# Inverse roots on ScalarE by logarithm and exponential, an earlier memory weight, a later key transpose and a respaced memory tail

## The chip, the cores and the metric

One core of a Trainium2 chip runs the whole kernel. The metric is device time in microseconds (us), from one launch; the median of three runs is compared. Five engines work side by side, each through its own list of instructions in order: TensorE (PE) multiplies matrices, ScalarE (ACT) applies functions to tiles, VectorE (DVE) and GpSimd (POOL) do elementwise work, and SyncE (SP) issues the transfers. An instruction that waits for another engine holds up everything behind it in its own list.

## The reference

The kernel computes one hybrid decoder layer for 1024 tokens of width 1024, with 256 memory tokens beside them:

```python
h = RMSNorm(x)                                       # x * rsqrt(mean(x^2) + 1e-6) * g
[pool_v | pool_gate | sb_q | sb_k | sb_v | sb_gate | mem_q | mem_gate] = h @ W_in
y_pool = pool_mixer(pool_v) * silu(pool_gate)        # windows 2, 4, 8, 16
y_sb   = stick_breaking(sb_q, sb_k, sb_v) * silu(sb_gate)          # 8 heads of 64
mk, mv = split(RMSNorm(mem) @ W_mem_kv)              # 4 heads of 64
s      = RMSNorm(mem_q) @ RMSNorm(mk).T / 8          # norms per head
y_mem  = softmax(s) @ mv * silu(mem_gate)
x      = x + concat(y_pool, y_sb, y_mem) @ W_out
```

Four kinds of norm need an inverse square root: of x (8 blocks of 128 tokens), of mem (2 blocks), of the memory keys and of the memory queries (per head).

## The kernel before

**Precision.** Every fp32 operand of a product is split into a high part, which ScalarE copies (`hh`, `wh_`), and the rest, which VectorE or GpSimd subtracts (`hl`, `wl_`). A product is three matmuls: high by high, low by high, high by low.

**Start.** The memory tokens are normed late (the factor `rm` is applied to the product), so the memory's keys and values `kv` can be multiplied as soon as `mem` and the first weights are there. The weights `w_mem_kv` come in four pieces, and SP issues them alternating with token blocks x0 to x3. `Norm.square` sums squares on ScalarE, `Norm.root` forms v = mean + eps on VectorE and v to the power -0.5 on GpSimd (L123), `newton` refines it by one step on VectorE, and `scale` multiplies the block. Then `h_step` transposes four blocks at once (L379, tile `tx`), so the first `tx` needs x0 to x3, and the first transposes of the second half need x4 to x7. `warm` puts unneeded matmuls into TensorE's list.

**Memory queries and keys.** Matmuls `u_mq` project the queries, for two pairs of heads and two halves of the tokens (`half[pr, th]`). `kv_root`, `kv_newton` give the keys' factor `r_k`, L447 the normed keys `kmn`, and `km_step` transposes them on TensorE (L469, tile `tk`). `mem_ss` sums squares of queries (`sp`, `v_q`, `r_q`), `mem_scale` makes the factor `qsc`. Roots of several columns go through `rsqrt_cols` (L95, on GpSimd).

**Memory attention.** `mem_main` lists 16 items (pair, head, two token blocks). Each is a score product `z_m` (L574, two tiles in turn), a maximum `nb_m` (L576, L580), the exponentials `pe_m` on ScalarE (L584), reciprocal (L592) and scaling of `pe_m` by GpSimd and VectorE (L595), a transpose `ta_m` (L493), its split `ah_m` (ScalarE, L503) and `al_m` (VectorE, L504), and the product `av` (L512). The transpose of an item comes three items after its scores, its `av` one later.

**Order.** TensorE's list is always the order of the code. `weave` mixes these steps with projections of the attention that follows (`u_k`, `u_v`, `u_g`): each step has a cost for TensorE, an occupation `occ` by which filling work is shared out, and a latency until what it gives is ready. VectorE's, ScalarE's and GpSimd's lists follow the code until `start.close()`; after that a scheduler orders them.

**After it** come four pairs of stick-breaking attention and the output product, which the change does not edit.

Of the kernel before, what the change touches and what calls it, by code (L numbers as in the profile page):

```python
# [8 lines left out]
F32 = mybir.dt.float32  # L9
F32R = mybir.dt.float32r  # L10
AF = mybir.ActivationFunctionType
# [3 lines left out]
P = 128  # L15
# [10 lines left out]
def layer_kernel(  # L26
# [48 lines left out]
    ctx.enter_context(tc.manual_schedule(engines={mybir.EngineType.PE}))  # L75


    ident = const.tile([P, P], F32, name="ident")
    make_identity(nc, ident[:])
    grow = pool.tile([P, P], F32, tag="pw", name="grow")[0:20, :]  # L80
    spare = const.tile([P, 2], F32, name="spare")
    rm = const.tile([P, 2], F32, name="rm")
    mhalf = const.tile([P, 16], F32, name="mhalf")
    nc.gpsimd.memset(mhalf[:], -0.5)
    bones = const.tile([P, 2], F32, name="bones")
    nc.gpsimd.memset(bones[:], 0.0)
    nc.gpsimd.memset(bones[0:HD, 0:1], 1.0)
# [2 lines left out]
    def rsqrt_cols(ss, n, inv, name):  # L90
        r = pool.tile([P, 16], F32, tag="rs", name=f"r_{name}", bufs=4)
        v = pool.tile([P, 16], F32, tag="rsv", name=f"v_{name}", bufs=2)
        t = pool.tile([P, 16], F32, tag="rst", name=f"t_{name}", bufs=2)
        nc.vector.tensor_scalar(v[:, :n], ss, inv, EPS, op0=ALU.mult, op1=ALU.add)
        nc.gpsimd.tensor_tensor(r[:, :n], v[:, :n], mhalf[:, :n], op=ALU.pow)  # L95

        def newton():
            nc.vector.tensor_tensor(t[:, :n], r[:, :n], r[:, :n], op=ALU.mult)
            nc.vector.tensor_tensor(t[:, :n], t[:, :n], v[:, :n], op=ALU.mult)
            nc.vector.tensor_scalar(t[:, :n], t[:, :n], -0.5, 1.5, op0=ALU.mult, op1=ALU.add)  # L100
            nc.vector.tensor_tensor(r[:, :n], r[:, :n], t[:, :n], op=ALU.mult)
            return r

        return newton

    class Norm:
# [11 lines left out]
                    sq[:], self.t, 1.0, self.t, op0=ALU.mult, op1=ALU.mult, accum_out=self.ss  # L118
                )

        def root(self):
            nc.vector.tensor_scalar(self.v, self.ss, 1.0 / D, EPS, op0=ALU.mult, op1=ALU.add)
            nc.gpsimd.tensor_tensor(self.r, self.v, mhalf[:, 0:1], op=ALU.pow)  # L123

        def newton(self, col=None):
            r, m = self.r, self.m
# [222 lines left out]
    def warm(dst, n):  # L349
        for i in range(n):  # L350
            nc.tensor.transpose(dst[:, 0:P], ident[:], ident[:])
# [17 lines left out]
    kb = [slot2(f"KB{i}", f"raw{i}") for i in range(2)]  # L369
    early_raw = [None, kb[1][:, 0:1024], kb[1][:, 1024:2048], kb[0][:, 0:1024], kb[0][:, 1024:2048], None]  # L370
    raw_kv = []
    for kk in range(4):
        raw_kv.append(load_raw(w_kv_v[:, 2 * kk : 2 * kk + 2, :], f"kv{kk}", early_raw[kk]))
        nc.sync.dma_start(xt[kk][:], xv[kk * P : (kk + 1) * P, :])

    def h_step(th, k):
        tp = ps(("z", "tr")[k % 2], f"tx{th}_{k}")
# [23 lines left out]
    def kv_split(kk):  # L401
        tags = (("wh", "wl"), ("wh", "wl"), ("qa0", "qb0"), ("KA0",))[kk]
        w_kv.append(split_w(raw_kv[kk], f"kv{kk}", tags, (nc.vector, nc.gpsimd)))

    def kv_step(kk):
        wh, wl = w_kv[kk]
        for j in range(2):
            k = 2 * kk + j
            wc = slice(j * 512, (j + 1) * 512)
            for w, m in ((wh, mh), (wh, ml), (wl, mh)):  # L410
                for i in range(2):
                    nc.tensor.matmul(
                        kvp[i][:],
                        m[:, k, i * P : (i + 1) * P],
                        w[:, wc],
                        start=(k == 0 and m is mh and w is wh),
                        stop=(k == KD - 1 and w is wl),
                    )
# [141 lines left out]
    def mem_main(mq, ys):  # L560
        items = [(pr, h, 2 * th + j) for th in range(2) for pr in range(2) for h in range(2) for j in range(2)]
        box = {}

        def qk(it):
            pr, h, j = it
            q, c0 = mq[pr][0]()[h], q_col(pr, 2 * j, h)
            rows = slice(h * HD, (h + 1) * HD)
            name = f"m{pr}_{h}_{j}"
            zp = ps("z", f"z_{name}")
            for i in range(2):  # L570
                tcol = slice((2 * j + i) * P, (2 * j + i + 1) * P)
                mc = slice(i * M, (i + 1) * M)
                for n in range(2):
                    nc.tensor.matmul(zp[:, mc], q[:, tcol], km[pr][:, 2 * n + h, :], start=(n == 0), stop=(n == 1))  # L574
            nb = pool.tile([P, 8], F32, tag="nb", name=f"nb_{name}", bufs=5)
            nc.vector.tensor_reduce(  # L576
                nb[:, 0:2], zp[:, 0:512].rearrange("p (i m) -> p i m", i=2), axis=AX.X, op=ALU.max, negate=True
            )
            pt = slot("be", f"pe_{name}")
            nc.vector.tensor_tensor(nb[:, 2:4], nb[:, 0:2], qsc[:, c0 : c0 + 3 : 2], op=ALU.mult)  # L580
            for i in range(2):
                col = c0 + 2 * i
                mc = slice(i * M, (i + 1) * M)
                nc.scalar.activation(  # L584
                    pt[:, mc],
                    zp[:, mc],
                    AF.Exp,
                    bias=nb[:, 2 + i : 3 + i],
                    scale=qsc[:, col : col + 1],
                    accum_out=nb[:, 4 + i : 5 + i],  # L590
                )
            nc.vector.reciprocal(nb[:, 6:8], nb[:, 4:6])  # L592
            for i in range(2):
                mc = slice(i * M, (i + 1) * M)
                (nc.gpsimd, nc.vector)[i].tensor_scalar_mul(pt[:, mc], pt[:, mc], nb[:, 6 + i : 7 + i])  # L595
            box[it] = pt

        def tr(it):
            pr, h, j = it
            pt = box[it]  # L600
            blocks = [[pt[:, i * M + b * P : i * M + (b + 1) * P] for i in range(2)] for b in range(2)]
            box[it] = a_t(blocks, f"m{pr}_{h}_{j}")

        def av(it):
            pr, h, j = it
            name = f"m{pr}_{h}_{j}"
            acc = av_half()
            a_v(acc, [vm[0][:, b, 2 * pr + h, :] for b in range(2)], box.pop(it), True, True)
            av_out(acc, h, name, ys[pr][h * HD : (h + 1) * HD, 2 * j * P : (2 * j + 2) * P])

        steps = []
        n = len(items)
        for t in range(n + 4):
            if t < n:
                steps.append(Step(0.44, lambda it=items[t]: qk(it), 1.5, 2.5, [("q", t - 3)], ("q", t)))
            if 0 <= t - 3 < n:
                steps.append(Step(0.43, lambda it=items[t - 3]: tr(it), 0.7, 2.4, [("q", t - 3)], ("t", t - 3)))
            if 0 <= t - 4 < n:
                steps.append(Step(0.44, lambda it=items[t - 4]: av(it), 0.3, 0.0, [("t", t - 4)]))
        return steps  # L620
# [154 lines left out]
        return Unit(r * P, f"pv{r}", evac), mix + [(KC, lambda th=th: out_step(th)) for th in range(2)]  # L775


    nc.scalar.activation(spare[:, 0:1], mhalf[:, 0:1], AF.Exp)
    start = ExitStack()
    start.enter_context(  # L780
        tc.manual_schedule(engines={mybir.EngineType.DVE, mybir.EngineType.Activation, mybir.EngineType.Pool})
# [23 lines left out]
    kv_split(0)  # L805
    m_evac(1)
    kv_step(0)
    m_evac(2)
    xn[0].square()
    kv_split(1)  # L810
    kv_step(1)
    m_evac(3)
    xn[0].root()
    xn[1].square()
    kv_split(2)
    xn[0].newton()
    xn[0].scale(nc.vector)
    kv_step(2)
    xn[1].root()
    xn[2].square()  # L820
    kv_split(3)
    xn[1].newton()
    xn[1].scale(nc.vector)
    xn[2].root()
    xn[3].square()
    xn[2].newton()
    xn[3].root()
    xn[2].scale(nc.vector)
    kv_step(3)
    for i in range(2):  # L830
        mn[i].root()
    raw_mq = [load_raw(w_in_v[:, :, 2560 + pr * P : 2560 + (pr + 1) * P], f"mq{pr}", early_raw[4 + pr]) for pr in range(2)]
    for i in range(4, 8):
        nc.sync.dma_start(xt[i][:], xv[i * P : (i + 1) * P, :])
    xn[3].newton()
    xn[3].scale(nc.vector, slice(0, 512))
    warm(ps("tr", "warm"), 4)
    w_mq = [(slot("wh", f"wh_mq{pr}", dt=F32R), slot("wl", f"wl_mq{pr}", dt=F32R)) for pr in range(2)]
    wc = (slice(0, 512), slice(512, 1024))

# [39 lines left out]
    for k in range(KD):  # L880
        half[0, 0][k][1]()
        half[1, 0][k][1]()
        if k + 3 < KD:
            h_step(0, k + 3)
        if k >= 5:
            h_step(1, k - 5)
        if k == 0:
            for i in range(2):
                mn[i].newton(col=rm[:, i : i + 1])
        if k <= 3:  # L890
            xn[4 + k].newton()
        if k < 2:
            xn[6 + k].square()
            xn[6 + k].root()
        if k <= 3:
            xn[4 + k].scale(nc.gpsimd if k < 2 else nc.vector)
        if k == 3:
            u_q[0].weights()
        if k == 4:
            kv_evac()  # L900
# [10 lines left out]
    for k in range(KD):  # L911
        half[0, 1][k][1]()
        if k == 0:
            kv_root()
            kv_newton()
        if k in (2, 3):
            mem_ss(k - 2, 0)
        if k == 4:
            mem_scale(0)
        if k in (6, 7):  # L920
            km_step(kmn, k - 6)
    for k in range(KD):
        half[1, 1][k][1]()
        if k == 1:
            u_k[0].weights()
        if k == 5:
            mem_ss(0, 1)
    start.close()
# [236 lines left out]
```

## Time and profile before

| quantity | value |
| --- | --- |
| median of 3 runs | 527.53 us (527.09 to 528.45) |
| the profiled execution, its own time | 532.06 us |
| its span, first to last instruction | 530.3 us |
| busy share: PE, DVE, ACT, POOL | 97%, 74%, 54%, 33% |
| mean granted clock of TensorE | 0.990 |

TensorE is busy nearly throughout, so the time is its work, its few waits, and the stretches in which its matmuls run slower. Times on the trace count from the start of the span. The profiled execution took 4.53 us more than the median; differences worked out on its trace are applied to the median.

### The profile page before, as it was taken

What the parts mean: (1) busy time and instruction counts of PE and PEld (TensorE: products, weight loads), DVE (VectorE), ACT (ScalarE), POOL (GpSimd) and SP (SyncE); (2) the same over time, 40 slices, a digit from 0 to 9 for tenths busy, and PEclk for the clock granted to TensorE, in tenths of its full rate; (3) what the DMA queues carried; (4) which work ended last, traced back from release to release, by engine and by line L of the source; (5) the groups of instructions that cost most, each with busy time, mean ns of one, the idle gap of its engine ahead of it and who ended that gap; (6) DMA issues with size and microseconds to landing.
All of it is one profiled execution on the core that took longest, in us unless ns stands there. A gap on an engine that the chain in (4) does not pass through costs nothing.

```text
span 530.3 us, 7458 instructions
## 1 busy us (share of the span) xinstructions
PE 515.0 (97%) x2720; PEld 433.1 (82%) x2720; DVE 393.3 (74%) x635; ACT 287.2 (54%) x549; POOL 177.0 (33%) x196
## 2 busy tenths in 40 slices
PE   7899898999899999999999999999999999999997
PEld 6678777888788888888888888888788888888886
DVE  4687667767567885876766776747988859999973
ACT  7787437667556564555545564535544539462400
POOL 3780464444122022022202210222345920034790
PEclk9999899999899999999999999999999999999999
DMA  8911012310110230123011113100110415413123
GB/s 298 339 45 41 0 54 66 81 40 1 40 41 1 80 81 0 41 58 91 13 40 41 41 40 80 40 25 19 40 41 0 159 45 195 159 41 119 41 110 127
DMA packets 37244, 37.25 MB, mean 70 GB/s; under 512 B 1990, under 2 KB 26840, under 8 KB 37208
## 3 DMA queue, kind: packets, MB, share of 16 engines
q1 hardware_dynamic: 37208, 36.78, 22.4%
q8 instruction: 21, 0.34, 0.3%
q14 instruction: 15, 0.12, 0.1%
HBM read 28.39 MB, written 4.19 MB: 61 GB/s over the span
## 4 chain that ended last, share of the span: by engine, by line
PE 85%; DVE 7%; ACT 2%; DMA 2%; POOL 2%; issue 1%; SPq 0%; ACTq 0%; POOLq 0%
PE av L512 8%; PE z L640 7%; PE ta L493 6%; PE u_g L209 6%; PE u_v L209 6%; PE u_k L209 5%; PE u_q L209 5%; PE u_g L206 3%; PE u_v L206 3%; PE u_mg L209 3%; PE oS L1047 3%; PE oS L1049 3%; PE u_pv L209 3%; PE oS L1048 3%; PE u_k L206 2%; PE u_q L206 2%
## 5 line engine op out<-in xcount | busy, mean ns | idle before, releaser
L648 DVE TENSOR_TENSOR_SCAN be<-be,later 128x128 f32<-128x128 f32 (+3 forms) x64 | 92.1, 1454 | 15.8 <-ACT be L644 14.8
L498 ACT ACTIVATE ah<-ta,mone 128x512 fp32r<-128x512 f32 (+1 forms) x80 | 51.6, 645 | 55.7 <-PE ta L493 54.9
L499 DVE SCALAR_TENSOR_TENSOR al<-ta,ah 128x512 fp32r<-128x512 f32 (+1 forms) x80 | 50.6, 632 | 23.3 <-ACT ah L498 22.2
L644 ACT ACTIVATE be<-z 128x128 f32<-128x128 f32 (+3 forms) x96 | 45.6, 490 | 32.3 <-PE z L640 30.8
L493 PE MATMUL ta<-ident,be 128*128 128x128 f32 x288 | 45.0, 273 | 0.0
L493 PEld LDWEIGHTS ta<-ident,be 128*128 128x128 f32 x288 | 34.8, 140 | 7.7 <-DVE be L648 0.7
L512 PEld LDWEIGHTS av<-ah,V_v 128*128 128x128 f32 x160 | 29.7, 188 | 6.7
L512 PE MATMUL av<-al,V_v 128*128 128x256 f32 (+1 forms) x160 | 31.7, 280 | 1.1 <-DVE al L499 1.1
L512 PE MATMUL av<-ah,V_v 128*128 128x256 f32 (+1 forms) x160 | 30.3, 271 | 0.0
L152 POOL TENSOR_TENSOR wl_k<-wr_k,wh_k 128x256 fp32r<-128x256 f32 x16 | 12.0, 782 | 47.9 <-ACT wh_k L148 47.9
L584 ACT ACTIVATE pe_m<-z_m,nb_m,qsc 128x256 f32<-128x256 f32 x32 | 17.8, 561 | 18.6 <-DVE nb_m L580 15.1
L206 PE MATMUL u_g<-hh,wh_g 128*128 128x512 f32 x64 | 27.7, 433 | 0.0
L206 PE MATMUL u_v<-hh,wh_v 128*128 128x512 f32 x64 | 27.1, 423 | 0.0
L595 POOL TENSOR_SCALAR pe_m<-pe_m,nb_m 128x256 f32<-128x256 f32 x16 | 16.9, 1056 | 29.8 <-DVE nb_m L592 25.7
L152 POOL TENSOR_TENSOR wl_g<-wr_g,wh_g 128x256 fp32r<-128x256 f32 x16 | 11.3, 741 | 45.7 <-ACT wh_g L148 30.8
L206 PE MATMUL u_k<-hh,wh_k 128*128 128x512 f32 x64 | 26.5, 414 | 0.0
L1047 PE MATMUL oS<-bs,hh 128*128 128x512 f32 (+1 forms) x68 | 25.9, 381 | 0.0
L1049 PE MATMUL oS<-bs,hl 128*128 128x512 f32 (+1 forms) x68 | 25.8, 379 | 0.0
L209 PE MATMUL u_g<-hh,wl_g 128*128 128x512 f32 x64 | 25.7, 402 | 0.0
L209 PE MATMUL u_g<-hl,wh_g 128*128 128x512 f32 x64 | 25.7, 402 | 0.0
L1048 PE MATMUL oS<-bs,hh 128*128 128x512 f32 (+1 forms) x68 | 25.6, 376 | 0.0
L209 PE MATMUL u_v<-hl,wh_v 128*128 128x512 f32 x64 | 25.3, 396 | 0.0
(312 smaller groups left out, 1497.5 us busy)
## 6 DMA issues: line engine op xcount, KB each, us to landing
x<-in_x_dram SPq DMA_DIRECT2D x8, 512.0 KB, 6.5
wr_q<-in_w_in_dram SPq DMA_DIRECT2D x4, 512.0 KB, 4.6
wr_k<-in_w_in_dram SPq DMA_DIRECT2D x4, 512.0 KB, 3.6
wr_v<-in_w_in_dram SPq DMA_DIRECT2D x4, 512.0 KB
KA_k<-KA_k SPq DMA_DIRECT2D x8, 256.0 KB, 5.4
KB_k<-KB_k SPq DMA_DIRECT2D x8, 256.0 KB, 4.6
wr_g<-in_w_in_dram SPq DMA_DIRECT2D x4, 512.0 KB, 4.7
xr<-in_x_dram SPq DMA_DIRECT2D x8, 256.0 KB, 4.6
```

The source lines that it names most:

```text
L206: nc.tensor.matmul(pt[:], wh[:, kc], hh[k][:, c], start=(k == 0), stop=False)
L209: nc.tensor.matmul(pt[:], w[:, kc], h[k][:, c], start=False, stop=(k == KD - 1 and n == 1))
L493: nc.tensor.transpose(tp[:, o : o + P], src, ident[:])
L498: nc.scalar.activation(ah[:, :w], tp[:, :w], AF.Identity, bias=mone[:, 0:1])
L499: nc.vector.scalar_tensor_tensor(al[:, :w], tp[:, :w], -1.0, f(ah[:, :w]), op0=ALU.add, op1=ALU.subtract)
L512: nc.tensor.matmul(av[:, 256 - bw : 256], vs[n], part[:, o : o + bw], start=(first and part is ah and n == 0), stop=(last and part is al a ...
L640: nc.tensor.matmul(zp[:, 0:w], q[h][:, tcol], k[h][:, n, s0 : s0 + w], start=(n == 0), stop=(n == 1))
L644: nc.scalar.activation(be[:, s0 : s0 + w], zp[:, 0:w], AF.Sigmoid, scale=-(HD**-0.5))
L648: nc.vector.tensor_tensor_scan(be[:, rev], be[:, rev], mask, 1.0, op0=ALU.mult, op1=ALU.max)
L1047: nc.tensor.matmul(bk[:, c], xh[:, tcol], wh[:, c], start=(n == 0), stop=False)
L1048: nc.tensor.matmul(bk[:, c], xh[:, tcol], wl[:, c], start=False, stop=False)
L1049: nc.tensor.matmul(bk[:, c], xl[:, tcol], wh[:, c], start=False, stop=(n == 3))
```

## The change

The dummy exponential at the start goes; instead table set 6 is loaded explicitly on ScalarE. The roots of x0 to x3, of the keys and of the queries are formed on ScalarE as exp(-0.5 ln(scale * ss + eps)), in two instructions; those of x4 to x7 and of mem stay on GpSimd. The second piece of the memory weights is issued ahead of x0, and x2 and x3 stand after the last piece. The start is written in another order, and 8 unneeded matmuls stand where 4 did. The roots of mem move from ahead of the first `u_mq` loop to its step 1, their Newton steps from step 0 to step 3. The two `km_step` calls move from the last two steps of `half[0, 1]` to steps 2 and 3 of `half[1, 1]`. In `mem_main`, transposes that come after the last scores get `occ` 2.2 instead of 0.7: 51 instead of 33 projection matmuls then stand after the last `z_m`, and 132 instead of 150 between the first and the last.

```diff
+    nc.scalar.add_instruction(
+        mybir.InstLoadActFuncSet(name=nc.get_next_instruction_name(), act_func_set_id=6, ins=[], outs=[])
+    )
...
+        nc.scalar.activation(r[:, :n], ss, AF.Ln, bias=eps[:, 0:1], scale=inv)
+        nc.scalar.activation(r[:, :n], r[:, :n], AF.Exp, scale=-0.5)
         nc.vector.tensor_scalar(v[:, :n], ss, inv, EPS, op0=ALU.mult, op1=ALU.add)
-        nc.gpsimd.tensor_tensor(r[:, :n], v[:, :n], mhalf[:, :n], op=ALU.pow)
...
-        def root(self):
+        def root(self, act=False):
+            if act:
+                nc.scalar.activation(self.r, self.ss, AF.Ln, bias=eps[:, 0:1], scale=1.0 / D)
+                nc.scalar.activation(self.r, self.r, AF.Exp, scale=-0.5)
             nc.vector.tensor_scalar(self.v, self.ss, 1.0 / D, EPS, op0=ALU.mult, op1=ALU.add)
-            nc.gpsimd.tensor_tensor(self.r, self.v, mhalf[:, 0:1], op=ALU.pow)
+            if not act:
+                nc.gpsimd.tensor_tensor(self.r, self.v, mhalf[:, 0:1], op=ALU.pow)
...
-    for kk in range(4):
+    for kk, blocks in enumerate(((), (0,), (1,), (2, 3))):
...
-                steps.append(Step(0.43, lambda it=items[t - 3]: tr(it), 0.7, 2.4, [("q", t - 3)], ("t", t - 3)))
+                steps.append(Step(0.43, lambda it=items[t - 3]: tr(it), 0.7 if t < n else 2.2, 2.4, [("q", t - 3)], ("t", t - 3)))
...
-    nc.scalar.activation(spare[:, 0:1], mhalf[:, 0:1], AF.Exp)
...
+    xn[0].root(True)
+    kv_split(2)
     m_evac(3)
...
-    warm(ps("tr", "warm"), 4)
+    warm(ps("tr", "warm"), 8)
...
-        if k == 0:
+        if k == 1:
+            for i in range(2):
+                mn[i].root()
+        if k == 3:
             for i in range(2):
                 mn[i].newton(col=rm[:, i : i + 1])
...
-        if k in (6, 7):
-            km_step(kmn, k - 6)
     for k in range(KD):
         half[1, 1][k][1]()
...
+        if k in (2, 3):
+            km_step(kmn, k - 2)
```

The first place is the start of ScalarE's list, before the change. `sq_x` sums squares of a token block, `wh_kv` copies the high part of memory weights, `mh` that of the transposed memory tokens.

```order
L115 ACTIVATE sq_x_234,ss_x_114<-x_97 128x1024
L157 ACTIVATE wh_kv_236<-raw_130 128x512 x2
L393 ACTIVATE mh<-tm_128,gcol 128x256 x2
L115 ACTIVATE sq_x_260,ss_x_115<-x_98 128x1024
L157 ACTIVATE wh_kv_262<-raw_130 128x512 x2
L115 ACTIVATE sq_x_285,ss_x_116<-x_99 128x1024
L157 ACTIVATE w_kv_287<-raw_129 128x512 x2
L115 ACTIVATE sq_x_297,ss_x_117<-x_100 128x1024
```

The same stretch of ScalarE's list after the change:

```order
L123 ACTIVATE sq_x_254,ss_x_117<-x_100 128x1024
L131 ACTIVATE ss_x_117<-ss_x_117,eps 128x1
L132 ACTIVATE ss_x_117<-ss_x_117 128x1
L169 ACTIVATE wh_kv_259<-raw_133 128x512 x2
L406 ACTIVATE mh<-tm_131,gcol 128x256 x2
L123 ACTIVATE sq_x_272,ss_x_118<-x_101 128x1024
L131 ACTIVATE ss_x_118<-ss_x_118,eps 128x1
L132 ACTIVATE ss_x_118<-ss_x_118 128x1
L169 ACTIVATE w_kv_289<-raw_132 128x512 x2
L123 ACTIVATE sq_x_297,ss_x_119<-x_102 128x1024
L131 ACTIVATE ss_x_119<-ss_x_119,eps 128x1
L132 ACTIVATE ss_x_119<-ss_x_119 128x1
```

A logarithm (L131) and an exponential (L132) of one column stand behind each sum of squares, and the second copy of memory weights has moved ahead of the first `sq_x`.

The second place is TensorE's list where the keys are transposed (`tk`). Before the change it stands in the first pair's queries:

```order
L206 MATMUL u_mq_1_602<-hh_86,wh_mq_335 128x512
L209 MATMUL u_mq_1_602<-hl_94,wh_mq_335 128x512
L209 MATMUL u_mq_1_602<-hh_86,wl_mq_336 128x512
L469 MATMUL tk_668<-ident,kmn 128x128 x2
L206 MATMUL u_mq_1_602<-hh_87,wh_mq_335 128x512
L209 MATMUL u_mq_1_602<-hl_95,wh_mq_335 128x512
L209 MATMUL u_mq_1_602<-hh_87,wl_mq_336 128x512
L469 MATMUL tk_689<-ident,kmn 128x128 x2
L206 MATMUL u_mq_1_700<-hh_80,wh_mq_337 128x512
```

After it, `tk` stands in the second pair's queries:

```order
L221 MATMUL u_mq_1_612<-hh_90,wl_mq_342 128x512
L218 MATMUL u_mq_1_688<-hh_83,wh_mq_343 128x512
...
L218 MATMUL u_mq_1_688<-hh_85,wh_mq_343 128x512
L221 MATMUL u_mq_1_688<-hl_93,wh_mq_343 128x512
L221 MATMUL u_mq_1_688<-hh_85,wl_mq_344 128x512
L482 MATMUL tk_708<-ident,kmn 128x128 x2
L218 MATMUL u_mq_1_688<-hh_86,wh_mq_343 128x512
```

Each `tk` has moved behind 12 further `u_mq` matmuls.

The third place is ScalarE's list at the end of the memory attention, where the last item's exponentials stand (`pe_m_1_3`). Before the change:

```order
L584 ACTIVATE pe_m_1_2_1401,nb_m_1_2_1399<-z_m_1_2_1394,nb_m_1_2_1399,qsc 128x256 x2
L503 ACTIVATE ah_m_1_3_1433<-ta_m_1_3_1428 128x512
L525 ACTIVATE avt_m_1_2_1445<-av_1440 64x256
L584 ACTIVATE pe_m_1_3_1458,nb_m_1_3_1456<-z_m_1_3_1451,nb_m_1_3_1456,qsc 128x256 x2
L503 ACTIVATE ah_m_0_2_1476<-ta_m_0_2_1471 128x512
L309 ACTIVATE V_v_1363<-tv_v_1_1480 128x8x64
```

After the change:

```order
L321 ACTIVATE V_v_1416<-tv_v_0_1417 128x8x64
L538 ACTIVATE avt_m_1_2_1429<-av_1424 64x256
L516 ACTIVATE ah_m_0_2_1457<-ta_m_0_2_1452 128x512
L597 ACTIVATE pe_m_1_3_1439,nb_m_1_3_1437<-z_m_1_3_1432,nb_m_1_3_1437,qsc 128x256 x2
L307 ACTIVATE vt_v_1_1464<-u_v_1_1360 128x512
L538 ACTIVATE avt_m_1_3_1473<-av_1468 64x256
```

The copy `ah_m` of item 0_2 stood behind the last exponentials and now stands ahead of them. In VectorE's list `al_m` of that item has likewise moved ahead of the last item's reciprocal. Of the 12 items from the fifth on, 8 had nothing between the maximum's last step and the reciprocal in VectorE's list; 5 have nothing there now.

## Rows read from the trace of the kernel before

**Rows 1.** Waits of PE in the whole span: line, released by; us in total, times, longest.

```profile
PE z_m L574 <- ACT pe_m L584: 2.1, 1, 2.1
PE ta_m L493 <- DVE al_m L504: 1.9, 1, 1.9
PE tk L469 <- DVE kmn L447: 1.6, 1, 1.6
PE tx L379 <- DVE x L133: 1.2, 1, 1.2
PE tx L379 <- DVE ss_m L122: 1.1, 1, 1.1
...
PE kv L412 <- ACT wh_kv L157: 0.7, 1, 0.7
```

**Rows 2.** Windows: width; busy (count) of PE, PEld, DVE, ACT, POOL; clock, DMA share, GB/s.

```profile
24.34:38.10 13.76, 13.71 (x69) 11.06 (x70) 10.87 (x29) 12.17 (x21) 11.97 (x14) 0.88 0.22 68
...
58.14:74.10 15.96, 15.95 (x71) 13.06 (x72) 8.60 (x24) 9.45 (x16) 7.98 (x6) 0.89 0.11 34
...
81.49:135.09 53.60, 53.60 (x316) 46.15 (x316) 38.55 (x92) 36.42 (x96) 24.97 (x33) 1.00 0.18 49
...
137.03:147.40 10.37, 10.37 (x53) 9.03 (x53) 4.91 (x9) 4.84 (x9) 0.02 (x1) 0.84 0.01 2
147.40:490.00 342.60, 341.42 (x1828) 288.19 (x1827) 268.59 (x371) 185.12 (x334) 85.30 (x90) 1.00 0.20 59
```

**Rows 3.** Timeline of ACT at the start: start, us, operation, idle before.

```profile
0.71 1.28 ACT L778 ACT_TABLE_LOAD   x1 [0.71 <-PEq L1152]
2.01 0.20 ACT L778 ACTIVATE spare<-mhalf 128x1 f32<-128x1 f32 x1
...
24.71 0.69 ACT L381 ACTIVATE hh<-tx,gcol 128x512 fp32r<-128x512 f32 x1 [1.94 <-PE tx L379]
```

**Rows 4.** Timeline of DVE at the start.

```profile
23.74 0.55 DVE L133 TENSOR_SCALAR x<-x,ss_x 128x512 f32<-128x512 f32 x1
...
30.42 0.27 DVE L127 TENSOR_SCALAR ss_m<-ss_m 128x1 f32<-128x1 f32 x1
...
37.23 0.81 DVE L133 TENSOR_SCALAR x<-x,ss_x 128x1024 f32<-128x1024 f32 x1
```

**Rows 5.** Timeline of PE, two matmuls that follow one another.

```profile
29.27 0.39 PE L209 MATMUL u_mq<-hl,wh_mq 128*128 128x512 f32 x1
29.51 0.39 PE L206 MATMUL u_mq<-hh,wh_mq 128*128 128x512 f32 x1
```

**Rows 6.** Timeline at the keys' root, POOL and DVE.

```profile
54.14 1.66 POOL L95 TENSOR_TENSOR r_k<-v_k,mhalf 128x8 f32<-128x8 f32 x1 [14.11 <-DVE v_k L94]
...
57.66 0.76 DVE L447 TENSOR_TENSOR kmn<-kvs,r_k 128x256 f32<-128x256 f32 x2
```

**Rows 7.** Timeline at the queries' roots, POOL and DVE.

```profile
71.85 2.90 POOL L95 TENSOR_TENSOR r_q<-v_q,mhalf 128x16 f32<-128x16 f32 x1 [3.28 <-DVE v_q L94]
74.72 2.84 POOL L152 TENSOR_TENSOR wl_v<-wr_v,wh_v 128x256 fp32r<-128x256 f32 x4
...
61.92 0.17 DVE L98 TENSOR_TENSOR t_q<-r_q 128x16 f32<-128x16 f32 x1 [3.02 <-POOL r_q L95]
...
74.78 0.70 DVE L98 TENSOR_TENSOR t_q<-r_q 128x16 f32<-128x16 f32 x1 [3.01 <-POOL r_q L95]
```

**Rows 8.** Timeline at the memory attention's end, ACT and DVE.

```profile
134.47 0.56 ACT L584 ACTIVATE pe_m<-z_m,nb_m,qsc 128x256 f32<-128x256 f32 x1 [2.17 <-PE av L512]
...
135.57 0.59 ACT L503 ACTIVATE ah_m<-ta_m 128x512 fp32r<-128x512 f32 x1
...
136.19 0.69 DVE L504 TENSOR_TENSOR al_m<-ta_m,ah_m 128x512 fp32r<-128x512 f32 x1
```

**Rows 9.** Waits of DVE from 81.49 to 135.09.

```profile
DVE nb_m L592 <- ACT pe_m L584: 11.7, 11, 1.4
DVE nb_m L576 <- PE z_m L574: 1.3, 3, 0.7
```

More of the change, by code (lines that the diff above doesn't have):

```diff
@@ L82, in layer_kernel @@
     rm = const.tile([P, 2], F32, name="rm")
-    mhalf = const.tile([P, 16], F32, name="mhalf")
+    mhalf = const.tile([P, 1], F32, name="mhalf")
     nc.gpsimd.memset(mhalf[:], -0.5)
+    eps = const.tile([P, 1], F32, name="eps")
+    nc.gpsimd.memset(eps[:], EPS)
     bones = const.tile([P, 2], F32, name="bones")
@@ L371, in layer_kernel @@
     raw_kv = []
-    for kk in range(4):
+    for kk, blocks in enumerate(((), (0,), (1,), (2, 3))):
         raw_kv.append(load_raw(w_kv_v[:, 2 * kk : 2 * kk + 2, :], f"kv{kk}", early_raw[kk]))
-        nc.sync.dma_start(xt[kk][:], xv[kk * P : (kk + 1) * P, :])
+        for i in blocks:
+            nc.sync.dma_start(xt[i][:], xv[i * P : (i + 1) * P, :])
     def h_step(th, k):
@@ L807, in layer_kernel @@
     kv_step(0)
+    kv_split(1)
     m_evac(2)
+    kv_step(1)
     xn[0].square()
-    kv_split(1)
-    kv_step(1)
+    xn[0].root(True)
+    kv_split(2)
     m_evac(3)
-    xn[0].root()
-    xn[1].square()
-    kv_split(2)
     xn[0].newton()
     xn[0].scale(nc.vector)
+    xn[1].square()
+    xn[1].root(True)
     kv_step(2)
-    xn[1].root()
-    xn[2].square()
     kv_split(3)
@@ L823, in layer_kernel @@
     xn[1].scale(nc.vector)
-    xn[2].root()
+    xn[2].square()
+    xn[2].root(True)
+    kv_step(3)
+    xn[2].newton()
     xn[3].square()
-    xn[2].newton()
-    xn[3].root()
+    xn[3].root(True)
     xn[2].scale(nc.vector)
-    kv_step(3)
-    for i in range(2):
-        mn[i].root()
     raw_mq = [load_raw(w_in_v[:, :, 2560 + pr * P : 2560 + (pr + 1) * P], f"mq{pr}", early_raw[4 + pr]) for pr in range(2)]
```

## The prediction

> **What bounds the kernel now.** I read the list of TensorE's waits first, since TensorE is the engine that hardly ever rests. In the longest window, 342.60 us of stick-breaking attention, it is busy for 341.42 us [rows 2]. The change edits nothing there, so what is won or lost before 147 us reaches the end. Only the first 147 us matter.
>
> Two things cost there. The first is waits: the list shows 2.1 us for a third `z_m`, 1.9 for a `ta_m`, 1.6 for a `tk`, 1.2 and 1.1 for two `tx`, and 0.7 for a `kv` [rows 1]. The second shows only in the windows. Three stretches have a granted clock of 0.88, 0.89 and 0.84, though TensorE is nearly 100% busy in them [rows 2]: width times the missing share is 13.76 x 0.12 = 1.65 us, 15.96 x 0.11 = 1.76 us and 10.37 x 0.16 = 1.66 us. Each is a short piece at 1.2 GHz among work at 2.4 GHz. The windows begin where a wait ends: for the last `tx`, the `tk`, the `ta_m`. The 2.1 us wait of `z_m` ended at 81.49, and the window behind it shows 1.00. So a wait was followed by a slow piece in three of four places, and I can't tell from the rows what spared the fourth.
>
> **The price of the new operation.** No row shows a logarithm with a bias on one column. The nearest is the one-column exponential at 2.01, 0.20 us [rows 3]; two of these make 0.40, which is the lower end. The upper end is two 512-column copies with a factor per partition, 0.69 each, so 1.38 [rows 3]. I take 0.5 for a pair, by the row that is nearest. The GpSimd roots cost 1.66 us for 8 columns and 2.90 for 16 [rows 6, 7].
>
> The Trainium skill's page ScalarE: Activation LUTs, section Rules for kernel authors, puts an operation with its bias in a tile at about 0.3 us and 0.83 ns an element. By that a pair is an estimated 0.6, the four at the start take 2.4 us, and the sum below would be some 0.4 smaller.
>
> **The change part by part.**
>
> *Start.* The piece of weights ahead of x0 removes the `kv` wait of 0.7 us, but the later pieces are copied later, because ScalarE has four pairs, 4 x 0.5 = 2.0 us, in a list that is nearly full there; I let the two cancel, and `kv` ends when it did (bounds: 0.7 either way). ScalarE had 1.94 us of idle time before its first `hh` [rows 3], so the 2.0 us delay of its list just fits. The GpSimd roots vanish from the chain to x3, so I expect x3's first half, scaled at 23.74 [rows 4], 0.3 to 0.9 us earlier, and the first `tx` with it. The four further unneeded matmuls fill idle time. This doesn't all reach the end: the same stage ends with x7, whose scaling stood at 37.23 and took 0.81 [rows 4], when TensorE was waiting for it. The chain to x7 begins with `hh` on ScalarE, so it moves up with the first `tx`; but the six small Newton steps of mem, from 0.15 to 0.27 us each with the first at 30.42 [rows 4], now stand directly ahead of x7's own on VectorE, and two GpSimd roots of mem stand ahead of x7's root. The gain is 0.1 to 0.8, and I take 0.4. If the first slow piece goes, TensorE merely arrives earlier at x7 and waits there; such a wait may be followed by a slow piece of its own, which I give even odds (three of four above had one), 0.5 x 1.65 = 0.8 us. The stage: 0.4 - 0.8 = -0.4 us, between -1.3 and +0.8.
>
> *Keys.* The `tk` stand 12 matmuls later. Two that follow one another start 0.24 us apart [rows 5], so 12 give 2.9 us. The root falls from 1.66 to 0.5, 1.2 us. Together 4.1 us cover the wait of 1.6, with TensorE's `u_mq` as the cover. If the keys' pair took 1.38, 3.2 would still do. The slow piece behind it goes too: 1.6 + 1.76 = 3.4 us, or 1.6 if the clock falls anyway. What needs `km` next, the first `z_m`, stands some 40 instructions later in TensorE's list.
>
> *Queries.* The second root falls from 2.90 to 0.5. That takes 2.4 us off the chain behind which the third `z_m` came 2.1 late [rows 1, 7]. Behind it, `t_q` took 0.70 us beside the subtraction of `wl_v` on GpSimd, where the same operation took 0.17 at 61.92 without such company [rows 7]. Four such steps cost 4 x 0.53 = 2.1 us too much. GpSimd is free earlier now, so the company may end earlier or meet the chain elsewhere. With it unchanged the chain still gains 2.4, 0.3 more than the wait: +2.1 us, between 0.5 (a pair at 1.38 and 0.7 more of company) and 2.1.
>
> *End of the memory attention.* The wait of 1.9 us ends with `al_m` at 136.19; ahead of it ScalarE did the last item's two exponentials, from 134.47 on, and only then `ah_m` at 135.57 [rows 8]. In the new order `ah_m` and `al_m` stand ahead of that item's exponentials and reciprocal, which takes the 1.1 us from 134.47 to 135.57 and the scaling out of the chain, and 18 further matmuls, 18 x 0.24 = 4.3 us, are spread over the tail. I count the wait as gone, and the slow piece behind it: 1.9 + 1.66 = 3.6 us, or 1.9 to 3.6.
>
> *Middle of the memory attention.* The 18 matmuls are missing between the scores. From 81.49 to 135.09 VectorE is busy 38.55 us [rows 2] and waits 11.7 + 1.3 us for exponentials and scores [rows 9], together 51.55 of 53.60. So 2.05 are spare, and 4.3 are taken away: 2.25 us too little, if VectorE's order were the same. It isn't: of 12 items only 5 instead of 8 now leave it idle between the maximum and the reciprocal, three waits of 11.7 / 11 = 1.1 us less, 3.2 us. Cost 0 to 2.25; I take 0.9, as the fillers won't fit everywhere.
>
> *Sum.* -0.4 + 3.4 + 2.1 + 3.6 - 0.9 = 7.8 us. On the profiled execution, 532.06 (span 530.3), that gives 524.3. The median of the runs shown is 527.53, 4.53 lower, and I apply the same gain to it: 519.7 us.
>
> **Rivals.**
>
> 1. *The slow pieces stay.* The waits go, but the clock falls at about the same places, as some wait is left near each. For: a wait of 2.1 had none behind it, so the wait alone doesn't decide. Against: each of the three pieces begins at a wait. Gain 7.8 - 1.76 - 1.66 = 4.4, so 523.1.
>
> 2. *The memory attention turns into an alternation of VectorE and ScalarE (the slower side).* In the new order `al_m`, 0.69 us [rows 8], stands between the maximum and the reciprocal of several items. If ScalarE has the exponentials ready sooner, it delays reciprocal, scaling and `ta_m` of each item. Over 13 items that is 9.0 us, and with the 2.25 above 11.2; less the 0.9 counted already, 10.3 more than in the sum: 527.53 - 7.8 + 10.3 = 530.0. It is slower than before from 0.6 us an item on (7.8 / 13). For: only 2.05 us are spare over the stage. Against: at present VectorE waits up to 1.4 us at that point [rows 9], more than 0.69, and the fillers stand in only 7 of 12 items.
>
> 3. *ScalarE is overloaded at the start.* With pairs at 1.38 its list slips by 4 x 1.38 = 5.5 us against 1.94 of room [rows 3]; x0 to x3 and then `hh` come 3.6 us late, of which the roots that left GpSimd give back about 0.9: 2.7 lost. That gives 519.7 + 2.7 + 0.4 = 522.8.
>
> 4. *The table changes between logarithm and exponential.* A load takes 1.28 us [rows 3]. If each of the seven pairs needed two, 2 x 4 x 1.28 = 10.2 us stand in the start and 2.6 in each of the other three roots. The start alone then loses 10.2 - 1.9 = 8.3, and the two waits that a shorter root removes stay in part: some 529 us. Against: ScalarE's list holds two loads before and after, none between the pairs.
>
> The Trainium skill's page ScalarE: Activation LUTs, section Table sets: the hidden batching unit, says that functions are loaded in named sets, and that one of them, natural_log_exp_and_others, holds both functions; by that rule no load falls between them and rival 4 costs nothing, which no run here shows yet. The same page, section What ACT_TABLE_LOAD costs, puts a load at about 2.7 us with its drain. The trace differs: the load took 1.28, and the next instruction stands at 2.01, 0.02 behind its end [rows 3]. By the page's figure the eight loads at the start would be an estimated 21.6 us instead of 10.2; the row decides here.
>
> **How the numbers follow.** My forecast has a chance of 0.52, with 517.3 to 521.9 as its own range (the best ends of the stages: -0.4 to +0.8 at the start, 0.9 to 0 in the middle; downward the bounds of start, queries and middle in part). Rival 1 has 0.23, rival 3 0.09, rival 2 0.08, rival 4 0.03; 0.05 is left for no effect at all, in which what is saved is waited for elsewhere. A difference of 0.3%, 1.6 us, is what a measurement of this kernel can tell from none. The forecast and rivals 1 and 3 are faster by more, 0.84; 0.07 lies within, 0.09 is slower. The range of 516.8 to 526.0 takes in the forecast, rivals 1 and 3, and leaves out the slower cases and half of the case without effect.
>
> **What would show it.** Right: no wait of TensorE above 0.5 us for `tk`, the third `z_m` or `ta_m`; clock 1.00 in the windows behind them; pairs of one column at about 0.5 us; two table loads. The first `tx` block ends before 24 us, and a wait of 1 to 2 us for x7 stands near 35 to 37 us if the first slow piece has gone. Wrong: new waits of TensorE for `al_m` or `pe_m` between the scores that add up to over 2.3 us, windows below 0.95 in new places, or a root pair over 1 us.

## The result and the profile after

The changed kernel took 523.99 us (median of 4 runs, 523.97 to 524.41), the kernel before 527.41 beside it (4 runs, 527.09 to 528.45): a ratio of 0.9934, with an interval of 0.9916 to 0.9951. So it is faster, by 3.4 us. The forecast was 7.8 us, to 519.7; the time lies inside the range of 516.8 to 526.0, and the gain falls 4.4 us short of the one forecast.

The profiled executions tell another story. The changed kernel's took 524.41 us with a span of 522.6 and a mean clock of 1.000, that of before 532.06 with 0.990. From one to the other the gain is 7.65 us, almost what was forecast. Both are true, and the difference between them is what this case is about.

TensorE's waits in the changed kernel, in the columns of [rows 1]:

```profile
PE tx L392 <- DVE x L145: 3.3, 2, 1.8
PE tm L363 <- POOL bones L94: 2.3, 1, 2.3
PE av L525 <- DVE al_m L517: 1.3, 2, 1.1
PE av L525 <- DVE al L512: 1.1, 1, 1.1
PE gps L373 <- issue: 0.9, 1, 0.9
PE kv L425 <- ACT wh_kv L169: 0.4, 1, 0.4
PE kv L425 <- ACT w_kv L169: 0.2, 1, 0.2
```

The waits for `tk`, the third `z_m` and `ta_m` are gone. What the reader is to see beside that: `tx` still waits 3.3 us, of which 1.8 is a new wait, and `av` waits 1.3 us for `al_m`, which is new too.

The windows of the changed kernel, cut at the same work as in [rows 2] (the row of nine `tx` behind the first waits to x7, x7 to the third `z_m`, to the last `z_m`, to the first attention scores, and the attention):

```profile
23.81:36.42 12.61, 12.55 (x68) 9.92 (x68) 9.22 (x27) 11.21 (x20) 10.75 (x14) 1.00 0.26 88
38.17:75.82 37.65, 37.65 (x199) 31.31 (x200) 27.96 (x58) 24.04 (x49) 8.29 (x12) 1.00 0.15 43
75.82:122.92 47.10, 45.84 (x275) 39.57 (x275) 33.94 (x84) 33.01 (x88) 20.94 (x27) 1.00 0.17 46
122.92:139.82 16.90, 16.90 (x98) 14.45 (x97) 9.98 (x20) 10.50 (x22) 5.03 (x8) 1.00 0.11 32
139.82:482.40 342.58, 341.39 (x1828) 288.33 (x1827) 268.54 (x372) 184.91 (x334) 85.17 (x90) 1.00 0.20 59
```

The clock is 1.00 in each. The last window is the untouched attention, 342.58 us against 342.60 [rows 2]: what is won before it does reach the end.

At what time the same instruction started, in three profiled executions (the middle one is the kernel before again, of the first experiment):

| start of | before | before, run again | changed |
| --- | --- | --- | --- |
| the last `tx` of all | 46.47 | 45.13 | 46.56 |
| the fourth `sp` | 70.41 | 67.51 | 66.93 |
| the third `z_m` | 81.49 | 78.16 | 75.82 |
| the last `z_m` | 131.01 | 127.64 | 122.92 |
| the attention's first scores | 147.40 | 144.08 | 139.82 |
| profiled execution's time | 532.06 | 528.81 | 524.41 |

### The profile page after: what moved, and what is told of

It reads as the page before. It is cut to its first block, busy times and chain, and to the rows that moved or that the text cites. A ratio compares the mean times of both kernels' runs of the same rounds, so it can differ in the third digit from the quotient of the medians.

```text
span 522.6 us, 7475 instructions
## 1 busy us (share of the span) xinstructions
PE 509.8 (98%) x2724; PEld 429.3 (82%) x2724; DVE 392.4 (75%) x635; ACT 289.8 (55%) x562; POOL 166.4 (32%) x190
## 4 chain that ended last, share of the span: by engine, by line
PE 85%; DVE 6%; ACT 5%; DMA 2%; issue 1%; ACTq 0%; DVEq 0%
PE av L525 8%; PE z L653 7%; PE ta L506 6%; PE u_g L221 6%; PE u_q L221 6%; PE u_v L221 5%; PE u_k L221 5%; PE u_g L218 3%; PE u_mg L221 3%; PE oS L1060 3%; PE u_q L218 3%; PE oS L1062 3%; PE u_pv L221 3%; PE oS L1061 3%; PE u_v L218 3%; PE u_k L218 2%
## 5 line engine op out<-in xcount | busy, mean ns | idle before, releaser
L221 PE MATMUL u_k<-hl,wh_k 128*128 128x512 f32 x64 | 25.3, 395 | 0.0
L221 PE MATMUL u_k<-hh,wl_k 128*128 128x512 f32 x64 | 25.3, 395 | 0.0
```

The costliest lines, as they stand in the source:

```text
L221: nc.tensor.matmul(pt[:], w[:, kc], h[k][:, c], start=False, stop=(k == KD - 1 and n == 1))
```

## The experiments

A slow piece is a short stretch in which TensorE's granted clock is the lower of its two levels, 1.2 instead of 2.4 GHz. Its size in us is the time that it costs: the width of a window times the share of the clock that is missing.

Theory A at first: the slow pieces belonged to the profiled execution alone, and the timed runs had none. Rival B: they are in the timed runs as well, and the gain was lost elsewhere. The runs showed a third case.

**The kernel before, again.** No edit.

> The kernel before, unchanged, run again with the granted clock of every run listed. Theory A (the three slow pieces of TensorE belong to the one profiled execution, and the timed runs had none): the timed runs show a clock of 0.998 to 1.000 and a span near 525.5 us, the time is 527.4 us, and the profiled execution may or may not have the slow pieces. Rival B (the slow pieces are in the timed runs too, and the gain of the change was lost somewhere else): the timed runs show a clock of about 0.990 as the profile of before did.

Measured: 528.61 us (12 runs, 526.99 to 531.68), and the kernel before beside it 529.28 (35 runs, 526.79 to 532.03). Neither A nor B: the clock changes from run to run, in steps. All 69 runs of the kernel before that were made beside the experiments:

| mean clock of the run | runs | time, median | lowest to highest |
| --- | --- | --- | --- |
| 0.999 or 1.000 | 15 | 527.24 | 526.77 to 528.16 |
| 0.996 or 0.997 | 27 | 528.46 | 527.30 to 529.61 |
| 0.993 or 0.994 | 11 | 530.50 | 529.28 to 531.37 |
| 0.990 | 16 | 531.77 | 531.01 to 532.23 |

One slow piece of about 1.7 us in 527 is 0.003 of the mean clock, so these are runs with none, one, two and three of them. Three cost 4.53 us by these medians, less than the 5.07 that the windows add up to. The profiled execution of before had three. The profiled execution of this experiment had one; its windows behind the same three waits as in [rows 2]:

```profile
23.93:37.00 13.07, 12.88 (x70) 10.10 (x71) 10.42 (x29) 11.83 (x21) 11.29 (x13) 1.00 0.22 70
56.80:72.00 15.20, 15.19 (x75) 12.53 (x76) 8.70 (x25) 9.25 (x16) 8.63 (x6) 1.00 0.12 36
133.71:144.08 10.37, 10.37 (x53) 9.09 (x53) 4.91 (x9) 4.84 (x9) 0.02 (x1) 0.84 0.01 2
```

TensorE's waits in this execution:

```profile
PE ta_m L493 <- DVE al_m L504: 2.0, 1, 2.0
PE z_m L574 <- ACT pe_m L584: 1.7, 1, 1.7
PE tk L469 <- DVE kmn L447: 1.6, 1, 1.6
PE tx L379 <- DVE x L133: 1.2, 1, 1.2
```

Ahead of the three windows TensorE waited 1.2, 1.6 and 2.0 us, about as in [rows 1], and the clock fell behind the third alone. So a wait of the same length was followed by a slow piece in one execution and not in another.

**The key transposes moved, alone.**

```diff
-        if k in (6, 7):
-            km_step(kmn, k - 6)
...
+        if k in (2, 3):
+            km_step(kmn, k - 2)
```

> The kernel before with the two key transposes alone moved to steps 2 and 3 of half[1, 1]; the keys' root stays on GpSimd. The 12 matmuls (2.9 us) cover the wait of 1.6 us by themselves. Theory A: 1.6 us less, 525.8 us. Rival B: 3.4 us less (the slow piece behind the wait goes too), 524.0 us. Rival C (the wait turns up again at the next place, the third z_m): no change, 527.4 us.

Measured: 530.47 us (12 runs), ratio 1.0034, interval 1.0011 to 1.0057: slower, nearest to rival C. The waits for `tk` and for the third `z_m` are gone, and a longer one stands between them. VectorE and then TensorE in this run:

```profile
61.79 0.69 DVE L98 TENSOR_TENSOR t_q<-r_q 128x16 f32<-128x16 f32 x1 [3.02 <-POOL r_q L95]
...
66.20 3.97 DVE L481 SCALAR_TENSOR_TENSOR km<-tk,gcol,km 64x256 fp32r<-64x256 f32 x8
70.20 0.17 DVE L553 COPY ssb<-sp 128x8 f32<-128x8 f32 x1
```

```profile
70.51 1.20 PE L551 MATMUL sp<-bones,sqq 128*128 128x2 f32 x5 [3.69 <-DVE ssb L553]
```

The copies of `km` now stand in VectorE's list behind the queries' Newton steps, which wait 3.02 us for GpSimd's root. The copy of `sp` behind `km` comes 3.69 us late for TensorE. That is about what the two waits that are gone had taken (1.6 and 1.7 in the execution above), so what makes the median slower is mostly the clock: it is 0.986 to 0.997 in these runs, and behind the new wait it is 0.75 from 70.50 to 82.10, a loss of 2.9 us.

**The roots of keys and queries on ScalarE, alone.** With the explicit table load and the tile `eps`:

```diff
+        nc.scalar.activation(r[:, :n], ss, AF.Ln, bias=eps[:, 0:1], scale=inv)
+        nc.scalar.activation(r[:, :n], r[:, :n], AF.Exp, scale=-0.5)
         nc.vector.tensor_scalar(v[:, :n], ss, inv, EPS, op0=ALU.mult, op1=ALU.add)
-        nc.gpsimd.tensor_tensor(r[:, :n], v[:, :n], mhalf[:, :n], op=ALU.pow)
```

> The kernel before with the roots of the keys and of the queries alone on ScalarE (logarithm and exponential, one table set); the start, the place of the key transposes and the tail stay. Theory A: the wait of the third z_m (2.1 us) goes and 1.1 of the 1.6 us of the key transpose, so 3.2 us less, 524.2 us. Rival B: the slow piece behind the key transpose goes as well if the wait left is short, up to 5 us less, 522.4 us. Rival C: the third z_m then waits for something else, under 1.5 us less.

Measured: 526.67 us (12 runs, 526.04 to 527.68), 2.6 below the 529.28 beside it, ratio 0.9953, interval 0.9933 to 0.9974. That median mixes runs with more and with fewer slow pieces. At equal clock, with one piece, eight runs have a median of 526.59 against 528.46 in the table, 1.9 less, where theory A had 3.2: `tk` waits 0.2 us still and the third `z_m` 0.7, 2.4 less together than in the first experiment. No run was at 0.999 or above: the wait at the tail, 1.9 us, is untouched, and in the profiled execution a slow piece stood behind it.

**The tail, alone.**

```diff
-                steps.append(Step(0.43, lambda it=items[t - 3]: tr(it), 0.7, 2.4, [("q", t - 3)], ("t", t - 3)))
+                steps.append(Step(0.43, lambda it=items[t - 3]: tr(it), 0.7 if t < n else 2.2, 2.4, [("q", t - 3)], ("t", t - 3)))
```

> The kernel before with the occupation of the late transposes alone raised from 0.7 to 2.2, so that 18 projection matmuls move from between the scores to behind the last. Theory A: the wait of 1.9 us at the end goes, new waits of about 1.3 us come in the middle (as the changed kernel's list shows for av on al_m), 0.6 us less, 526.8 us. Rival B: with the slow piece 2.3 us less, 525.1 us. Rival C: the scores' stage is held up more than the tail gains, 528 us or more.

Measured: 528.76 us (12 runs), ratio 0.9981, interval 0.9952 to 1.0009: inconclusive as it stands. At a clock of 0.999 or above, its four runs have a median of 526.79, against 527.24: 0.45 us, near the 0.6 of theory A but not clear of noise, as the two groups overlap (526.25 to 527.36, 526.77 to 528.16). The tail's wait is gone, and the list shows what came for it:

```profile
PE av L512 <- DVE al_m L504: 1.3, 2, 1.1
```

**The changed kernel, again.** No edit.

> The changed kernel as it is, run again beside many runs of the kernel before. Theory (the kernel before has none to three slow pieces of 1.66 to 1.76 us from run to run, the changed kernel has none): the changed kernel stays within 0.5 us at 524.0 with a clock of 0.999 to 1.000, the kernel before spreads from 526.8 to 532.0 with a median near 529.3, so the gain is 5.3 us against that median and 2.8 against its best runs. Rival: the changed kernel spreads as well once it is run often, over 2 us, and its earlier runs were lucky.

Measured: 523.99 us (6 runs, 523.90 to 525.13), every run at a clock of 1.000; beside it the kernel before 528.58 (17 runs), ratio 0.9901, interval 0.9862 to 0.9939. The theory holds but for one run, 525.13, which is 1.1 us above the median at the same clock: the changed kernel's clock is 0.999 or 1.000 in all 10 runs, so none has a slow piece of that size. Its gain is 3.3 us against runs of before with none (527.24), 4.6 against the median here and 7.8 against runs with three.

**The new start, alone.** The changed kernel with the three edits above undone:

```diff
-        nc.scalar.activation(r[:, :n], ss, AF.Ln, bias=eps[:, 0:1], scale=inv)
-        nc.scalar.activation(r[:, :n], r[:, :n], AF.Exp, scale=-0.5)
...
+        nc.gpsimd.tensor_tensor(r[:, :n], v[:, :n], mhalf[:, :n], op=ALU.pow)
...
+        if k in (6, 7):
+            km_step(kmn, k - 6)
...
-        if k in (2, 3):
-            km_step(kmn, k - 2)
```

> The kernel before with the new start alone (roots of x0 to x3 on ScalarE, the order of loads and of the start, 8 unneeded matmuls, mem's roots and Newton steps later); keys, queries and tail stay. Theory: x7 is late by about 1.8 us, so the best runs are 1.4 us slower than the best of before, 528.2 us, with no slow piece at the start but with those behind the waits for keys and the tail. Rival (the forecast's own term): 0.4 us slower to 0.4 faster than before in the median, 529 us.

Measured: 529.78 us (12 runs), ratio 1.0007, interval 0.9979 to 1.0035, inconclusive. At a clock of 0.999 or above, four runs have a median of 528.26. That is 1.0 above 527.24, but 0.3 above the five runs of before at this clock beside them, 528.00. So these times alone put the start between 0.3 and 1.0, less than the 1.4 expected; the traces decide further below.

**Roots and key transposes together, on the old start.** The edits of the key transposes and of the roots at once.

> The kernel before with the roots of keys and queries on ScalarE and the key transposes moved, both at once; the start and the tail stay. Moved alone the transposes cost 1.2 us, the roots alone gave 2.6. Theory (the moved transposes put VectorE's copy of km behind the second pair's squares, and the wait of 3.7 us behind it was the slow GpSimd root in front; with the root short it goes): 1.0 us less than the roots alone, 525.7 us. Rival (the two simply add up): 527.9 us.

Measured: 524.28 us (6 runs, 523.31 to 524.54), 2.4 below the roots alone. The two don't add up: the same move cost 1.2 us in the median with the GpSimd root and gives 2.4 with the short one. TensorE doesn't wait for `sp`, `tk` or `z_m` in this run, so the 0.2 and 0.7 us that the roots alone had left are gone; and none of these runs has two slow pieces, where four of the 12 with the roots alone had.

**All but the new start.** The edits of the key transposes, of the roots and of the tail at once.

> The kernel before with three parts of the change at once, the roots of keys and queries on ScalarE, the moved key transposes and the later projection matmuls at the tail; only the new start is left out. Theory (the parts add up, and the new start costs 1.4 us at equal clock): 524.0 - 1.4 = 522.6 us, and with the waits for keys and tail gone the clock is 0.999 or 1.000 in all but a run or two. Rival (the start is needed by the rest, for instance through GpSimd being free earlier): 524 us or more.

Measured: 523.43 us (6 runs, 523.08 to 524.48), between the theory and its rival. Four of six runs are at 0.999 or above, 523.08 to 523.45, so the new start costs 0.5 to 0.9 us against 523.99. With the start alone it was 0.3 to 1.0.

**Unneeded matmuls in the waits of the kernel before.**

```diff
+        if pr == 0:
+            warm(tp, 13)
...
-    warm(ps("tr", "warm"), 4)
+    warm(ps("tr", "warm"), 14)
```

> The kernel before with 13 unneeded 128-column matmuls ahead of the first key transpose (in the tile that the transpose overwrites) and 14 instead of 4 ahead of the first token transposes, so that TensorE works through about 1.5 and 1.1 us of its waits there; nothing is made earlier. Theory (a slow piece of TensorE follows its idle time): the slow piece at the keys never comes, at the start seldom, no run shows a clock of 0.990 where about a quarter of the runs of before do, the best runs stay at 526.8 to 527.2 and the median falls to about 528. Rival (the slow pieces come by themselves, whatever TensorE does): the spread and the share of 0.990 stay, median as the kernel before.

Measured: 527.06 us (12 runs, 526.38 to 528.60), ratio 0.9977, interval 0.9956 to 0.9998. Seven runs are at 0.999 or 1.000, five at 0.996 or 0.997, none below, where 27 of 69 runs of before are below. TensorE at the keys, and the windows behind the three waits:

```profile
55.27 1.58 PE L351 MATMUL tk<-ident 128*128 128x128 f32 x13
57.02 0.66 PE L471 MATMUL tk<-ident,kmn 128*128 128x128 f32 x2 [0.16 <-DVE kmn L447]
```

```profile
24.14:37.00 12.86, 12.67 (x69) 9.88 (x70) 10.21 (x29) 11.94 (x21) 11.09 (x12) 1.00 0.23 72
57.02:72.00 14.98, 14.97 (x74) 12.33 (x75) 8.60 (x24) 8.40 (x15) 8.55 (x6) 1.00 0.13 36
133.42:143.78 10.36, 10.36 (x52) 8.98 (x53) 4.82 (x9) 4.84 (x9) 0.02 (x1) 0.84 0.01 2
```

At the start two waits follow one another, and only the first is filled; the second still stands ahead of the first window:

```profile
24.14 1.20 PE L379 MATMUL tx<-ident,x 128*128 128x128 f32 x9 [1.16 <-DVE x L133]
```

The keys come no earlier than before, and the waits are only filled, yet the median is 1.2 us below the 528.30 beside it, with an interval that just leaves out 1. No run has more than one piece. In the profiled execution it stood behind the unfilled `ta_m`; where the other four had theirs isn't shown. So less idleness of TensorE brought fewer falls of the clock. It isn't the whole rule: the changed kernel waits 1.50 and 1.75 us and has none.

**Mem's Newton steps behind x7.**

```diff
-        if k == 1:
+        if k == 2:
             for i in range(2):
                 mn[i].root()
-        if k == 3:
+        if k == 4:
             for i in range(2):
                 mn[i].newton(col=rm[:, i : i + 1])
```

> The changed kernel with the roots of mem one step later (behind x7's root on GpSimd) and its Newton steps one step later (behind x7's scaling on VectorE). Theory (the start loses 1.4 us because x7's Newton step and scaling stand behind the six Newton operations of mem): the wait of 1.8 us before the transposes of the second half goes, 1.5 to 1.8 us less than the changed kernel, 522.3 us. Rival 1 (x7 is late for another reason, the chain of ScalarE): under 0.3 us. Rival 2 (the keys' and values' copies, which need the mem factor, hold ScalarE up and the wait comes back at a later transpose): 523.5 us or more.

Measured: 522.13 us (6 runs, 521.90 to 522.29), 1.9 below the changed kernel, which has 523.99 in the same comparison; ratio to before 0.9859, interval 0.9825 to 0.9893. This is the fastest version. VectorE in this run:

```profile
34.23 0.27 DVE L139 TENSOR_SCALAR ss_x<-ss_x 128x1 f32<-128x1 f32 x1
34.54 0.15 DVE L140 TENSOR_SCALAR ss_x<-ss_x 128x1 f32<-128x1 f32 x1
34.73 0.81 DVE L145 TENSOR_SCALAR x<-x,ss_x 128x1024 f32<-128x1024 f32 x1
35.46 0.75 DVE L395 SCALAR_TENSOR_TENSOR hl<-tx,gcol,hh 128x512 fp32r<-128x512 f32 x1
36.12 0.27 DVE L139 TENSOR_SCALAR ss_m<-ss_m 128x1 f32<-128x1 f32 x1
```

x7 is scaled from 34.73 on, mem's steps follow, and of the 3.3 us of `tx` 1.5 are left. The edit moves the roots on GpSimd as well; but in the changed kernel x7's root there was done at 33.79, before the Newton steps began at 35.00, so the steps are what held x7 up. Rival 2 is answered by the time: the copies that need mem's factor wait 2.4 us on ScalarE, and no `tx` waits for them.

## Why the prediction was wrong, and where it held

**The step that failed first** is the last line of the sum: "The median of the runs shown is 527.53, 4.53 lower, and I apply the same gain to it". Of the 7.8 us forecast, 1.76 + 1.66 = 3.4 were slow pieces. They were in the profiled execution, which had three, and hardly in the runs behind the median, 527.09 to 528.45, which by their times in the table above had none or one (their clock is not on record). A gain of 3.4 us that the compared runs had no part in was taken from them all the same. The clue stood on the page: 5.07 us of slow pieces, and a profiled execution 4.53 us above the median. The pieces were the difference. Taken off once, the forecast was 7.8 - 3.4 = 4.4, or 523.1. That this lies within 0.9 us of the measured time is partly luck: 0.8 of the sum was set aside for a slow piece at x7 that never came. With no slow piece on either side the terms give 0.4 + 1.6 + 2.1 + 1.9 - 0.9 = 5.1, and 3.25 was measured at equal clock (527.24 - 523.99). Two terms were mis-sized, the start and the memory attention.

**Start, forecast -0.4 (0.4 gained, 0.8 in a slow piece at even odds), measured about -1.0 without one.** The forecast spoke of mem's Newton steps ahead of x7's and let them take no more than 0.1 to 0.2 us off the gain (0.3 to 0.9 became 0.1 to 0.8). VectorE and TensorE in the changed kernel:

```profile
35.00 0.27 DVE L139 TENSOR_SCALAR ss_m<-ss_m 128x1 f32<-128x1 f32 x1
...
36.35 0.54 DVE L142 TENSOR_TENSOR rm<-ss_m 128x1 f32<-128x1 f32 x1
36.82 0.26 DVE L139 TENSOR_SCALAR ss_x<-ss_x 128x1 f32<-128x1 f32 x1
37.11 0.15 DVE L140 TENSOR_SCALAR ss_x<-ss_x 128x1 f32<-128x1 f32 x1
37.30 0.81 DVE L145 TENSOR_SCALAR x<-x,ss_x 128x1024 f32<-128x1024 f32 x1
```

```profile
38.17 0.33 PE L392 MATMUL tx<-ident,x 128*128 128x128 f32 x1 [1.75 <-DVE x L145]
```

The six steps take 1.8 us, from 35.00 to 36.82, and TensorE waits 1.75 for x7. That the scaling stands where it did, 37.30 against 37.23 [rows 4], had looked like a neutral start; but 37.23 was itself late. In the kernel before without a slow piece at the start (the first experiment) x7 was scaled here:

```profile
35.70 0.99 DVE L133 TENSOR_SCALAR x<-x,ss_x 128x1024 f32<-128x1024 f32 x1
```

Of the 1.53 us between the two, 0.4 stood already at the row of nine `tx`, 24.34 against 23.93, and 0.8 is the scaling of x6, which took 1.61 us in one execution and 0.81 in the other. How much of it the slow piece brought about isn't shown. The row that bounded the term came from an execution in which this stretch ran late. That TensorE would meet a wait of 1 to 2 us at x7 was forecast; that no slow piece follows it was left at even odds, and none came.

**The price of a pair** was 0.5 by the nearest row. It is 0.53, from the start of the logarithm to the end of the exponential:

```profile
13.41 0.29 ACT L131 ACTIVATE ss_x<-ss_x,eps 128x1 f32<-128x1 f32 x1
13.74 0.20 ACT L132 ACTIVATE ss_x<-ss_x 128x1 f32<-128x1 f32 x1
```

Between them stands no table load, and the whole list has two, at 0.72 and 134.80, as forecast. That settles rivals 3 and 4. The Trainium skill's page ScalarE: Activation LUTs, section Table sets: the hidden batching unit, agrees: one load serves both functions. Its section Rules for kernel authors puts the operation with the bias at about 0.3 us, and the row has 0.29.

**Keys, forecast 3.4 (1.6 of wait); queries, forecast 2.1.** Right in place, and in size where the piece was there: from the last `tx` to the fourth `sp` 3.6 us between the first and third columns of the table, to the third `z_m` 2.2 more. Without slow pieces the two together give 527.24 - 523.31 = 3.9 by the one run of both on the old start at 0.999, against 1.6 + 2.1 = 3.7. What the forecast missed, though it costs the whole change nothing, is that the move needs the short roots: it counted the 2.9 us of matmuls as cover and looked at TensorE's list alone, not at VectorE's, where the copies of `km` come to stand behind the queries' root. With that root on GpSimd the move alone gained nothing.

**End and middle of the memory attention, forecast 3.6 - 0.9, without the piece 1.9 - 0.9 = 1.0, measured 0.3 to 0.45.** The mechanism at the end is as told. ScalarE in the changed kernel:

```profile
125.49 0.60 ACT L516 ACTIVATE ah_m<-ta_m 128x512 fp32r<-128x512 f32 x1 [1.06 <-PE ta_m L506]
126.33 0.56 ACT L597 ACTIVATE pe_m<-z_m,nb_m,qsc 128x256 f32<-128x256 f32 x1 [0.24 <-DVE nb_m L593]
```

`ah_m` stands ahead of the last exponentials, the reverse of [rows 8], and TensorE no longer waits for `ta_m`. The middle was mis-sized, 1.3 us of new waits instead of 0.9, most of it in one place:

```profile
92.19 0.50 PE L525 MATMUL av<-al_m,vm 128*128 128x256 f32 x2 [1.05 <-DVE al_m L517]
```

**Rivals.** The time of rival 1 (the slow pieces stay), 523.1, came near, and its mechanism is refuted: the changed kernel has none. They were subtracted where they hadn't been. Rival 2 priced 11.2 us in the memory attention; the new waits for `al_m` there are 1.3.

**The sum at equal clock.** By the times, -1.0 (start alone) + 3.9 (keys and queries) + 0.45 (tail) = 3.35 us, and the changed kernel measured 3.25. So close an agreement is luck: one term rests on a single run, and the runs of before at 0.999 or above have medians of 527.15, 528.00 and 527.08 beside the three sets of experiments. The traces bear the terms out. The stretches between the same instructions, in profiled executions without a slow piece in that stretch:

| stretch | without the part | with it | gain |
| --- | --- | --- | --- |
| up to the row of nine `tx` | 24.04 (mean of 7) | 23.54 (mean of 3) | 0.5 |
| from there to the last `tx` of all | 21.20 to 21.22 (5) | 22.74 to 22.76 (3) | -1.55 |
| to the third `z_m`, keys and queries | 33.03 (before, run again) | 29.26 (changed) | 3.8 |
| to the attention's first scores, tail | 64.29 (roots and keys) | 64.00 (changed) | 0.3 |

That makes about 3.0 us, and it places the loss of the start: the row of nine `tx` does begin about half a microsecond earlier, as forecast, and three times as much is lost behind it, at x7.

Two bounds of the prediction don't come out of their own terms: the lower bound of the queries is 2.90 - 1.38 - 0.7 = 0.8 and not 0.5, and the lower end of its own range is 519.7 - 1.2 - 0.9 = 517.6 and not 517.3. Nothing of the result hangs on them.

## What to carry to other kernels

A profiled execution that lies above the median of the timed runs holds something that those runs don't have; find it before any gain read from it is subtracted from the median, and compare runs at equal clock. A moment at which something is ready may only be late because the stretch before it was slow, so a bound read there is too kind to what the change puts in front. A move that takes its cover from one engine can still stand behind another engine's wait: look in every list for what it now stands behind.

## What had not been expected of the hardware

TensorE's clock falls to its lower level behind a wait in some executions and not in others, with the same program and waits of the same length: behind the 1.6 us of `tk` it fell in one profiled execution of the kernel before and not in the other. Over all profiled executions here, of whichever version, that have the wait, a slow piece followed the 1.9 to 2.0 us of `ta_m` in five of seven, the 1.6 of `tk` in one of four, the 1.0 to 2.2 of the third `z_m` in one of five (with the start alone: a clock of 0.97 from 79.80 to 130.80), and the two waits of 1.0 and 1.2 us at the first `tx` in three of seven. So the `z_m` that the prediction found spared was not safe. The mean clock of a run counts these pieces, about 0.003 each.

In the changed kernel, waits of 1.50 us (first `tx`) and 1.75 us (x7) came with no slow piece in any of 10 runs; what makes that difference was not settled. Matmuls whose results nobody needs, put into two of the waits, took 1.2 us off the median of the kernel before.
